# Where the last head keeps the previous head's gated output

## The chip, the cores and the metric

The kernel runs on one core of a Trainium2 chip. Its time is the device time of one launch in microseconds (us). The kernel before took 1392.94 us, the median of three runs (1392.48 to 1395.17).

## The reference

One step of a two-layer decoder on 512 prompt tokens and 32 sample tokens (8 sequences of 4), 544 columns in all, with 1024 features. Layer 0 mixes with a short gated convolution, layer 1 with a retention of four heads; each layer ends with a gated feed-forward network (FFN) of 2816 hidden features. What matters here is the retention of layer 1 and the start of its FFN:

```python
x = x + m                                   # m: the mixer's output
x = x + swiglu(rmsnorm(x, norm_ffn[i]), ffn_w_gate[i], ffn_w_up[i], ffn_w_down[i])
# retention mixer, per head h (dk = 256, dv = 512):
q, k, v, g = jnp.split(x @ w_in, ...)       # q and k then turned by rotary
o, S = retention_chunkwise(q, k, v, s0)     # scores, inner and cross products, new state
of = (o - mean(o)) * rsqrt(var(o) + eps)
out = (silu(g) * of * gn_g) @ w_out         # summed over the heads into x
```

## The kernel before

**Number format.** Every product is made of three matmuls: an operand `a` is split into a high part `ah` (float32r, made by ScalarE, ACT) and a low part `al = a - ah` (made by VectorE, DVE), and `a*b` is `ah*bh + ah*bl + al*bh` on TensorE (PE). The helper `split` (L206 ACT, L207 DVE) does one such split. So each step on PE waits for an ACT instruction and a DVE instruction that follows it.

**Layout.** `x` is kept transposed as 8 tiles of 128 features by 544 columns. Its parts for the products of the retention are `xh[0..7]` and `xl[0..7]`, all in one resident tile `parts`. A projection by an output matrix (`project`, L190) walks over 4 feature tiles ("k tiles") of its input with 6 matmuls each, 24 in all.

**A head.** The loop over `h` in 0..3 starts with `value` (V = x @ w_v from `xh`, `xl`, weights in four pieces c = 0..3, each piece over two of the eight feature tiles: c = 0 reads tiles 0 and 1, c = 1 tiles 2 and 3, and so on). Behind c = 0 PE transposes the last parts of the previous head's normalized output, and DVE multiplies them into that head's gate tile (L1612, L1616): it then holds the gated output of the previous head, `older`. Behind c = 1, `qk_split` splits the keys and queries, `keys` transposes the keys, and `held_parts` splits the gated output of the previous head. Then follow `state`, `scores`, `inner`, the sample updates (L1669, L1687, L1693) and the store of the states. Between these, `fill` puts projections of the previous head's gated output through its output matrix, `held_project(h, n)` for n = 0..7, to give PE work while the other engines prepare. In heads 1 and 2 all eight are done inside the head. In head 3, n = 2, 3, 4, 5 are done inside it, n = 0 and 1 at its end, and n = 6 and 7 inside `last_project`, which projects head 3's own output: in the order 0, 1, 4, 5, 2, 3, 6, 7, with `held_project` ahead of n = 6 and of n = 7. Each n ends with `residual(n)`, the DVE addition into `x[n]` (L318).

**What follows.** `ffn(1)` prepares from each `x[kt]` the seven operand blocks of a Strassen-like product: `operand(kt)` scales `x[kt]` into a tile `f` (L884, ACT), subtracts blocks of `f` (L325 to L333, DVE), and splits the blocks into `oh` and `ol` (L206, L207). It runs over kt in the order 0, 1, 4, 5, 2, 3, 6, 7 after the program's order of the residuals; a pair kt, kt + 4 shares one `f`, and there are two `f` buffers. The first job's products then read `oh[0..3]` and `ol[0..3]` (L426, PE): block 0 and block 1 of all four pairs (24 matmuls), then three products over the first three pairs (27 matmuls), then what needs the fourth pair's rest.

**Memory.** Pools are stacks of tiles; a pool opened after others are closed takes the same addresses, and each of its tiles waits for the tiles that it covers (`reuse_waits="tile"`). Behind the same resident pools lie, in the retention, with bytes per partition from the common base: `vp` (`vyh` and `vyl`, 2 x 8704), `qp` (`qkhl1` 8704, `qkhl0` 8192, `vs` 2048), `kp` (`rot1` 36352 to 40704, `rt0` to 42880, `gt` 42880 to 47232), `tp`, which has its `gate` at 72448 to 81152, and three state tiles `S`; in the FFN: `gu` (4 x 4352), the weight tiles `w2`, `w4`, `h2`, `l2`, `h4`, `l4` (18432 together), the two `f` (35840 to 41280 and 41280 to 46720), then `oh`/`ol` of the pairs, 7616 each, from 46720.

**Where the previous head's split output lies.** `held_parts` writes the high parts to two tiles of `kp`, tags `gt` and `rot1`, and the low parts to `gate` of `tp` (heads 2 and 3). The gated output itself lies in `qkhl1` of `qp` (heads 1 to 3), the same buffer in which `qk_split` puts the split keys; so for heads 2 and 3 (`QAHEAD`) the keys are split after `held_parts` has read the gate tile, while heads 0 and 1 split them first.

**Order.** The program's order is not the order on the engines: a planner places each instruction by the program's order and by when its own cost model finds it ready; each engine then runs its list strictly in that order. `tc.issue_after(ins)` forces an instruction behind another. A `weave` is a generator that `project` advances once after each k tile, so that other work is issued there; `last_product` is the last projection matmul issued so far.

Of the kernel before, what the change touches and what calls it, by code (L numbers as in the profile page):

```python
# [9 lines left out]
F32R = mybir.dt.float32r  # L10
# [3 lines left out]
P = 128  # L14
D = 1024
KT = D // P
SEQ = 512
# [8 lines left out]
NH = 4  # L26
# [18 lines left out]
AHEAD = (1, 2)  # L45

QAHEAD = (2, 3)
# [8 lines left out]
def hybrid_decode_kernel(ctx: ExitStack, tc: tile.TileContext, a: dict, o: dict):  # L56
# [7 lines left out]
    def nm(s):  # L64
        uid[0] += 1
        return f"{s}_{uid[0]}"
# [65 lines left out]
    xh, xl = [[parts[:, i * KT + k, :] for k in range(KT)] for i in range(2)]  # L132
# [72 lines left out]
    def split(dh, dl, src):  # L205
        h = nc.scalar.activation(dh, src, AF.Copy)  # L206
        last_low[0] = nc.vector.tensor_sub(dl, src, dh.bitcast(F32))  # L207
        return h
# [194 lines left out]
    class Job:  # L403
# [10 lines left out]
        weave = iter(())  # L414
# [130 lines left out]
    with ExitStack() as c0:  # L545
# [7 lines left out]
        st = mask_p[:, : KT * NB * 2].rearrange("p (k b s) -> p k b s", k=KT, b=NB)  # L553
# [204 lines left out]
        y = taps(0)  # L758
# [527 lines left out]
    with ExitStack() as c2:  # L1286
# [3 lines left out]
        qp = c2.enter_context(tc.tile_pool(name="rtq", bufs=1, reuse_waits="tile"))  # L1290
# [97 lines left out]

        def qk_split(h, st, which):
            r = st["rot"][which]  # L1390
            both = qp.tile([P, 2, 2, SEQ], F32R, tag=f"qkhl{which}", name=nm("qkhl"), bufs=1)
            th, tl = both[:, 0, :, :], both[:, 1, :, :]
            split(th, tl, r[:, :, :SEQ])
            st["qk"[which]] = (th, tl)

# [7 lines left out]
        def value(h, st):  # L1403

            pv = [bank() for _ in range(4)]
            pvs = psum()
            raw = []
            for c in range(4):
                wh, wl = load_piece(a["rtv"][h, c], 2 * DV, keep=raw)
                for k2 in range(2):  # L1410
                    kt = 2 * c + k2
                    cw = slice(k2 * DV, (k2 + 1) * DV)
                    for tt in range(4):
                        ts_, out = token_tiles(tt), pv[tt]
                        nc.tensor.matmul(out, xh[kt][:, ts_], wh[:, cw], start=(kt == 0), stop=False)  # L1415
                        nc.tensor.matmul(out, xh[kt][:, ts_], wl[:, cw], start=False, stop=False)  # L1416
                        last = nc.tensor.matmul(out, xl[kt][:, ts_], wh[:, cw], start=False, stop=(kt == KT - 1))  # L1417
                if c == 0 and "pair" in st:
                    last_product[0] = last
                    st["pair"]()  # L1420
                if c % 2:

                    with tc.issue_after(last.ins):
                        for g in range(4):
                            kt = 2 * c - 2 + g
                            nc.tensor.matmul(  # L1426
                                pvs[g * NS : (g + 1) * NS, 0, :], xs[:, kt, :],
                                raw[kt // 2][:, kt % 2 * DV : (kt % 2 + 1) * DV],
                                start=(c == 1), stop=(c == 3), skip_group_check=True,
                            )  # L1430
                if c == 1:
                    if h not in QAHEAD:
                        with tc.issue_after(last_normal[0].ins) if h else ExitStack():
                            qk_split(h, st, 1)
                    qk_split(h, st, 0)
                    gs = st["gs"] = one.tile([P, NS], F32, tag="gs", name=nm("gs"), bufs=1)
                    nc.vector.tensor_mul(
                        by_sequence(gs), by_sequence(R[:, 1, HT - NS :]), fq[:, h, :].unsqueeze(1).to_broadcast([P, NB, DS])
                    )
                    sample_scores(h, st, pvs[:, 1, :])  # L1440
                    for dt in range(2):
                        qsrc = st["rot"][0][:, dt, SEQ:].rearrange("p (g r s) -> p g r s", g=4, r=2)
                        for r in range(2):
                            nc.vector.scalar_tensor_tensor(
                                qm[:, dt, :, r, 4 * r : 4 * r + 4], qsrc[:, :, r, :], _gamma(h) ** 4,
                                gs.rearrange("p (g r s) -> p g r s", g=4, r=2)[:, :, r, :], op0=ALU.mult, op1=ALU.mult,
                            )
                    keys(h, st, pvs[:, 1, P:])
                    if h:
                        held_parts(h, older)  # L1450
                    if h in QAHEAD:
                        qk_split(h, st, 1)
            v4 = tp.tile([P, 2, DV], F32R, tag="mid", name=nm("v4"), bufs=1)
            nc.scalar.activation(v4[:, 0, :], pvs[:, 0, :], AF.Copy, scale=fv[:, 4, h : h + 1])
            nc.vector.scalar_tensor_tensor(
                v4[:, 1, :], pvs[:, 0, :], fv[:, 4, h : h + 1], v4[:, 0, :].bitcast(F32), op0=ALU.mult, op1=ALU.subtract
            )

            def placed():
                with tc.issue_after(last_product[0].ins) if h in AHEAD else ExitStack():  # L1460
                    for i in range(2):
                        nc.tensor.matmul(pvs[:, 1, :], put, v4[:, i, :], start=(i == 0), stop=(i == 1))
                vt = kp.tile([P, DV], F32R, tag="rt0", name=nm("vt"), bufs=1)
                vs = st["vs"] = qp.tile([P, DV], F32R, tag="vs", name=nm("vs"), bufs=1)
                v2_split[0] = nc.scalar.activation(vt, pvs[:, 1, :], AF.Copy, scale=sign[:, 0:1])
                nc.vector.scalar_tensor_tensor(
                    vs, pvs[:, 1, :], place[:, 1:2], vt.bitcast(F32), op0=ALU.mult, op1=ALU.add
                )

            st["placed"] = placed  # L1470
            if h not in AHEAD:
                placed()
            vh = vp.tile([P, 4, DV], F32R, tag="vyh", name=nm("vh"), bufs=1)
            vl = swapped(h == 1, [P, 4, DV], F32R, "vl")
            for tt in range(4):
                nc.scalar.activation(vh[:, tt, :], pv[tt], AF.Copy, scale=fv[:, tt, h : h + 1])
                nc.vector.scalar_tensor_tensor(
                    vl[:, tt, :], pv[tt], fv[:, tt, h : h + 1], vh[:, tt, :].bitcast(F32),
                    op0=ALU.mult, op1=ALU.subtract,
                )  # L1480
            st["v"] = (vh, vl)
# [50 lines left out]
        def gate_tile(st, n):  # L1532
            return st["gate"][n // 2][:, n % 2, :] if len(st["gate"]) > 1 else st["gate"][0][:, n, :]
# [176 lines left out]
        held = {}  # L1710

        def held_parts(h, st):

            yh = [kp.tile([P, 2, T], F32R, tag=t, name=nm("oldh"), bufs=1) for t in ("gt", "rot1")]
            yl = swapped(h > 1, [P, 4, T], F32R, "oldl")
            for i, t in enumerate(yh):
                c = slice(2 * i, 2 * i + 2)
                split(t, yl[:, c, :], st["gate"][0][:, c, :])
            held["y"] = [t[:, n, :] for t in yh for n in range(2)], [yl[:, n, :] for n in range(4)]

        def held_project(h, n, add=True, single=False, weave=()):

            if n % 2 == 0:
                held["w"] = load_piece(a["rtout"][h - 1, n // 2], 2 * 4 * P, adding=not add and n > 0)
            pt = [bank(), bank()] if single else psum()
            steps = (step() if step else None for step in weave)
            project(pt, *held["w"], n % 2 * 4 * P, *held["y"], last=add, weave=steps)
            if add:
                residual(n, pt)
            else:  # L1730
                held[n] = pt
# [13 lines left out]
        st = qk_places(0)  # L1745
# [4 lines left out]
        older = None  # L1750
        for h in range(NH):
            more = h + 1 < NH

            def fill(place):

                for n in {1: ((0,), (1,), (2,), (3, 4)), 2: ((0,), (1,), (2,), (3, 4)), 3: ((), (2,), (), (3,))}.get(h, ((),) * 4)[place]:
                    held_project(h, n)
                    if n == 0:
                        st["placed"]()
# [60 lines left out]
            if h == 0:  # L1820
                qk_project(h + 1, nxt, 0, 1, inside)
            elif more:
                nc.sync.dma_start(nxt["rot"][0], q_made[h + 1])
                held_project(h, 6, single=True, weave=(None, inside))
                held_project(h, 7)
            else:
                held_project(h, 5, single=True)
                held_project(h, 0, False, single=True, weave=iter((inside,)))
# [127 lines left out]
```

## Time and profile before

| what | value |
|---|---|
| median of three runs | 1392.94 us |
| profiled execution: time, span | 1393.6 us, 1391.8 us |
| mean granted TensorE clock | 0.995 |
| PE busy | 1376.3 us (99%) |
| DVE busy | 1141.3 us (82%) |
| ACT busy | 832.5 us (60%) |
| POOL busy | 216.0 us (16%) |
| head 3's `value` to the end of `last_project` | about 914 to 1017 us |
| first matmuls of `ffn(1)` | 1017.65 us |

The profile page gives busy times, the span in 40 slices of 34.8 us, and the chain of work that ended last. Views of the trace give instructions in order of time (start, duration, engine, line, operation, output<-inputs, and in brackets the idle time before it and what ended it), groups by line, waits, and windows with busy time, granted clock (1.00 is full speed) and DMA share. In groups and timelines `oldh` and `oldl` are the split output of the previous head, `yh` and `yl` that of head 3 itself. A few per cent of the matmul records are missing.

### The profile page before, as it was taken

How to read it: one execution, taken by the hardware profiler on the slowest of the kernel's cores; microseconds unless marked ns; L12 is line 12 of the kernel's file. 1: busy time of each engine (PE TensorE's matmuls, PEld its weight loads, DVE VectorE, ACT ScalarE, POOL GpSimd, SP SyncE). 2: the span in 40 equal slices, each digit the busy share in tenths (PEclk: the TensorE clock that was granted, in tenths of full speed). 3: DMA queues.
4: the chain of work that ended last, by engine and by line, in shares of the span. 5: the costliest groups of instructions: out<-in, count | busy, mean ns of one | idle time of the engine just before them, and what ended most of it. 6: DMA issues, size and time to landing. Idle time of an engine off the chain costs nothing.

```text
span 1391.8 us, 26526 instructions
## 1 busy us (share of the span) xinstructions
PE 1376.3 (99%) x10396; PEld 1313.6 (94%) x10396; DVE 1141.3 (82%) x1938; ACT 832.5 (60%) x1304; POOL 216.0 (16%) x255
## 2 busy tenths in 40 slices
PE   9999999999999999999999999999979999999998
PEld 9999999999999999999977787877979999999998
DVE  6998889888989878789877666676779898988875
ACT  7666567776677557676642413222567767667654
POOL 0111012121222104111110000000111222221212
PEclk9999999999999999999999999999989999999999
DMA  6566347777776745678666655556736767777752
GB/s 223 122 163 160 110 120 176 155 173 182 153 191 151 173 98 163 182 201 204 185 243 218 207 205 192 205 205 231 194 73 164 171 166 175 153 180 172 160 115 87
DMA packets 100733, 236.69 MB, mean 170 GB/s; under 512 B 9952, under 2 KB 34032, under 8 KB 100096
## 3 DMA queue, kind: packets, MB, share of 16 engines
q1 hardware_dynamic: 68608, 168.37, 37.9%
q0 software_dynamic: 29264, 57.40, 24.1%
q10 hardware_dynamic: 2736, 9.23, 1.7%
q8 instruction: 81, 1.33, 0.4%
q14 instruction: 44, 0.36, 0.1%
HBM read 193.74 MB, written 29.53 MB: 160 GB/s over the span
## 4 chain that ended last, share of the span: by engine, by line
PE 96%; DVE 2%; DMA 1%; ACT 1%; issue 0%; SPq 0%; DVEq 0%; ACTq 0%
PE sm L426 45%; PE mm L426 17%; PE mm L190 14%; PE sm L190 5%; PE sm L1416 2%; PE sm L1417 2%; PE sm L1415 2%; PE sm L178 2%; PE sm L179 1%; PE sm L180 1%; PE sm L1669 1%; DMA x<-in_xT_dram 1%; PE mm L1426 1%; PE mm L1597 1%; PE mm L1687 0%; DVE ol L207 0%
## 5 line engine op out<-in xcount | busy, mean ns | idle before, releaser
L426 PE MATMUL sm<-oh,wh 128*128 128x272 f32 x872 | 252.5, 290 | 6.5 <-ACT oh L206 6.5
L426 PE MATMUL sm<-ol,wh 128*128 128x272 f32 x872 | 252.1, 289 | 1.0 <-DVE ol L207 0.9
L426 PE MATMUL sm<-oh,wl 128*128 128x272 f32 x872 | 251.3, 288 | 0.0
L206 ACT ACTIVATE h<-w 128x512 fp32r<-128x512 f32 (+3 forms) x175 | 141.1, 806 | 92.7 <-PE mm L426 85.8
L207 DVE TENSOR_TENSOR l<-w,h 128x512 fp32r<-128x512 f32 (+3 forms) x175 | 158.4, 906 | 23.7 <-ACT h L206 21.8
L339 ACT ACTIVATE wh<-w 128x1024 fp32r<-128x1024 f32 (+1 forms) x138 | 138.2, 1001 | 62.4 <-PE sm L426 45.4
L426 PEld LDWEIGHTS sm<-oh,wh 128*128 128x128 f32 x872 | 165.1, 189 | 7.4 <-ACT oh L206 7.2
L426 PEld LDWEIGHTS sm<-ol,wh 128*128 128x128 f32 x872 | 164.6, 189 | 1.9 <-DVE ol L207 1.8
L426 PEld LDWEIGHTS sm<-oh,wl 128*128 128x128 f32 x872 | 164.9, 189 | 0.0
L426 PE MATMUL sm<-parts,wh 128*128 128x272 f32 x768 | 148.3, 288 | 0.0
L206 ACT ACTIVATE wh<-w 128x1024 fp32r<-128x1024 f32 (+3 forms) x74 | 63.2, 860 | 126.8 <-PE mm L190 86.7
L342 POOL DMA_DIRECT2D wl<-in_ffgu_dram x87 | 81.3, 935 | 340.6 <-ACT wl L341 161.1
L426 PEld LDWEIGHTS sm<-parts,wh 128*128 128x128 f32 x768 | 120.3, 188 | 0.0
L426 PE MATMUL mm<-oh,h 128*128 128x272 f32 x404 | 116.2, 288 | 0.0
L426 PE MATMUL mm<-oh,l 128*128 128x272 f32 x404 | 115.7, 286 | 0.0
L426 PE MATMUL mm<-ol,h 128*128 128x272 f32 x404 | 115.4, 286 | 0.0
L426 PE MATMUL sm<-parts,wl 128*128 128x272 f32 x384 | 110.4, 288 | 0.0
L341 ACT ACTIVATE wl<-wh 128x512 fp32r<-128x512 f32 (+1 forms) x178 | 106.2, 596 | 2.3
L340 DVE TENSOR_TENSOR wl<-w,wh 128x512 fp32r<-128x512 f32 (+1 forms) x138 | 89.8, 651 | 16.7 <-ACT wh L339 16.5
L426 PE MATMUL sm<-oh,h 128*128 128x272 f32 x292 | 85.7, 294 | 0.0
L426 PE MATMUL sm<-ol,h 128*128 128x272 f32 x292 | 84.9, 291 | 0.0
L426 PE MATMUL sm<-oh,l 128*128 128x272 f32 x292 | 84.6, 290 | 0.0
(395 smaller groups left out, 3795.4 us busy)
## 6 DMA issues: line engine op xcount, KB each, us to landing
w<-in_ffgu_dram SPq DMA_DIRECT2D x66, 512.0 KB
wl<-in_ffgu_dram POOLq DMA_DIRECT2D x87, 256.0 KB, 5.3
S<-in_rets_dram SPq DMA_DIRECT2D x16, 1024.0 KB
out_rets_dram<-S SPq DMA_DIRECT2D x16, 1024.0 KB
w<-in_ffdn_dram SPq DMA_DIRECT2D x36, 384.0 KB
cb<-in_ffgu_dram SPq DMA_DIRECT2D x22, 512.0 KB
w<-in_cvin_dram SPq DMA_DIRECT2D x21, 512.0 KB
wl<-in_ffdn_dram POOLq DMA_DIRECT2D x48, 192.0 KB, 4.7
```

Of the source, the lines that this page charges most:

```text
L178: nc.tensor.matmul(out, lh, rh, start=start, stop=False, skip_group_check=True)
L190: last_product[0] = nc.tensor.matmul(half(pt, hf)[:, :HT], w[:, c], act[k][:, hf * HT : (hf + 1) * HT], start=(first and k == ks[0] and i ...
L206: h = nc.scalar.activation(dh, src, AF.Copy)
L207: last_low[0] = nc.vector.tensor_sub(dl, src, dh.bitcast(F32))
L339: nc.scalar.activation(wh, w, AF.Copy)
L340: last_mixed[0] = nc.vector.tensor_sub(wl[:, :n], w[:, :n], wh[:, :n].bitcast(F32))
L341: minus = nc.scalar.activation(wl[:, n:], wh[:, n:].bitcast(F32), AF.Copy, scale=-1.0)
L342: nc.gpsimd.dma_start(wl[:, n:], src[:, 1, :] if len(src.shape) == 3 else src[:, n:], accum_op=ALU.add)
L426: last = nc.tensor.matmul(out, w[:, c], b, start=(first and j == 0 and i == 0), stop=(j == len(self.ks) - 1 and i == 2), skip_group_check= ...
L1415: nc.tensor.matmul(out, xh[kt][:, ts_], wh[:, cw], start=(kt == 0), stop=False)
L1416: nc.tensor.matmul(out, xh[kt][:, ts_], wl[:, cw], start=False, stop=False)
L1417: last = nc.tensor.matmul(out, xl[kt][:, ts_], wh[:, cw], start=False, stop=(kt == KT - 1))
```

## The change

Three edits in head code.

1. For the last head the keys are split ahead of the queries, as in heads 0 and 1, and not into `qkhl1` but into two tiles of `kp` with the tags `gt` and `rot1`, which in heads 1 and 2 hold the high parts of the previous head's output. The condition `h not in QAHEAD` becomes `h != 2`.
2. For the last head `held_parts` is no longer called behind c = 1 of `value`. It is called in `fill`, ahead of the head's first `held_project` (n = 2, between the two calls of `state`), and it writes in four splits of 544 columns into `xh[0..3]` and `xl[0..3]`, which no later step of the layer reads as x's parts. No tile of `kp` or `tp` holds them then.
3. In heads 1 and 2 the generator given to `held_project(h, 6)` has one more empty step, so that `inside` (the transposes of the third token tile's normalized output, and the last state update) is issued after the third k tile and not after the second.

```diff
         def qk_split(h, st, which):
             r = st["rot"][which]
-            both = qp.tile([P, 2, 2, SEQ], F32R, tag=f"qkhl{which}", name=nm("qkhl"), bufs=1)
-            th, tl = both[:, 0, :, :], both[:, 1, :, :]
+            if which and h == NH - 1:
+                th, tl = [kp.tile([P, 2, SEQ], F32R, tag=t, name=nm("khl"), bufs=1) for t in ("gt", "rot1")]
+            else:
+                both = qp.tile([P, 2, 2, SEQ], F32R, tag=f"qkhl{which}", name=nm("qkhl"), bufs=1)
+                th, tl = both[:, 0, :, :], both[:, 1, :, :]
             split(th, tl, r[:, :, :SEQ])
...
                 if c == 1:
-                    if h not in QAHEAD:
+                    if h != 2:
                         with tc.issue_after(last_normal[0].ins) if h else ExitStack():
                             qk_split(h, st, 1)
                     qk_split(h, st, 0)
...
-                    if h:
+                    if h in AHEAD:
                         held_parts(h, older)
-                    if h in QAHEAD:
+                    if h == 2:
                         qk_split(h, st, 1)
...
         def held_parts(h, st):
 
+            if h == NH - 1:
+                for n in range(4):
+                    split(xh[n], xl[n], gate_tile(st, n))
+                held["y"] = xh[:4], xl[:4]
+                return
...
                 for n in {1: ((0,), (1,), (2,), (3, 4)), 2: ((0,), (1,), (2,), (3, 4)), 3: ((), (2,), (), (3,))}.get(h, ((),) * 4)[place]:
+                    if h == NH - 1 and n == 2:
+                        held_parts(h, older)
                     held_project(h, n)
...
-                held_project(h, 6, single=True, weave=(None, inside))
+                held_project(h, 6, single=True, weave=(None, None, inside))
                 held_project(h, 7)
```

## The prediction

> **What bounds the kernel now.** I read the page first (its slices), then the waits of PE, then PE in order of time around its longest wait, then the granted clock by windows.
>
> ```profile
> PE   9999999999999999999999999999979999999998
> PE sm L426 <- ACT oh L206: 6.5, 3, 5.5
> PE sm L426 <- DVE ol L207: 0.9, 2, 0.7
> PE sm L1597 <- DVE yn L1574: 0.4, 2, 0.2
> ```
>
> PE is the bound nearly everywhere; only slice 30 (1009 to 1044 us) has a hole. 7.4 us of PE's waits are for `oh` and `ol`, the operands of `ffn(1)`, and 0.4 us for the third token tile's normalized output in heads 1 and 2. Inside head 3 PE waits for nothing that this view lists. So a change to heads can pay or cost in three places: at the two waits of 0.2 us, in new waits, or at the hand-over from `last_project` to `ffn(1)`. That place in order of time, then by windows:
>
> ```profile
> 1017.00 0.41 PE L190 MATMUL mm<-yh,wl 128*128 128x272 f32 x2
> 1017.65 0.40 PE L426 MATMUL sm<-oh,wh 128*128 128x272 f32 x1 [0.24 <-ACT oh L206]
> ...
> 1020.09 0.29 PE L426 MATMUL sm<-oh,l 128*128 128x272 f32 x1
> 1025.92 0.59 PE L426 MATMUL sm<-oh,wh 128*128 128x272 f32 x1 [5.54 <-ACT oh L206]
> ...
> 1026.00:1035.70 9.70, 8.69 (x32) 7.41 (x33) 8.91 (x17) 6.67 (x11) 0.00 (x0) 0.50 0.06 11
> 1035.70:1046.00 10.30, 10.30 (x86) 10.30 (x85) 7.66 (x14) 5.12 (x8) 2.09 (x2) 1.00 0.50 130
> ...
> 1021.00:1022.00 1.00, 0.00 (x0) 0.00 (x0) 1.00 (x3) 1.00 (x3) 0.00 (x0) 1.00 0.02 2
> 1022.00:1023.00 1.00, 0.00 (x0) 0.00 (x0) 1.00 (x2) 1.00 (x2) 0.00 (x0) 0.52 0.00 0
> ```
>
> A window row gives PE, weight loads, DVE, ACT, POOL (busy us), then clock, DMA share, GB/s. The longest wait costs more than its 5.54 us: the clock falls about 1.6 us after the last matmul ends (1020.38 to 1022.0) and stays at 0.50 until 1035.7. PE's 8.69 busy us there would be 4.35 at full clock. The hand-over therefore loses 7.4 + 4.35 = **11.75 us**.
>
> Why are the operands late? Views by tile of `oldh` and of x, the timeline of ACT, and the chain of waits:
>
> ```profile
> L190 PE MATMUL mm<-oldh,wl x48: 285/288/291, 947.4 to 1014.1; 128*128 128x272 f32 x48
> 990.35 0.79 DVE L318 TENSOR_TENSOR x<-x,sm 128x272 f32<-128x272 f32 x2 [1.10 <-PE sm L190]
> L318 DVE TENSOR_TENSOR x<-x,mm x7: 714/721/722, 993.4 to 1017.4; 128x544 f32<-128x544 f32 x7
> 1014.19 1.06 ACT L339 ACTIVATE wh<-w 128x1024 fp32r<-128x1024 f32 x1 [4.91 <-PE mm L190]
> 1015.15 0.73 ACT L884 ACTIVATE f<-x,vec 128x544 f32<-128x544 f32 x1
> 1029.12 0.64 DVE ol L207
> 1029.81 1.27 PE sm L426 x4
> ```
>
> `x[0]` is final at 991.14, yet its first scaling into `f` starts at 1015.15, 24 us later and right behind the last matmuls on `oldh` (1014.1). The buffers explain it: `f` lies at 35840 to 41280 and 41280 to 46720, over `rot1` and `gt` of `kp`, which hold `oldh`; `ol` of the second pair and `oh` of the third lie over `gate` of `tp`, which holds `oldl`. All are read by `held_project(3, 7)`. From there the chain runs through ACT and DVE until PE resumes.
>
> **The change, part by part.**
>
> *Buffers (edits 1 and 2).* In head 3 `gt` and `rot1` then hold split keys, last read by the scores, and `gate` of `tp` is last read in head 2. The moved work is the groups of 1014.5 to 1036 us; the room is the window ahead:
>
> ```profile
> L207 DVE TENSOR_TENSOR ol<-f,oh 128x544 fp32r<-128x544 f32 (+1 forms) x12 | 9.2, 814 | 0.7 <-ACT oh L206 0.7
> L325 DVE TENSOR_TENSOR f<-f 128x272 f32<-128x272 f32 x4 | 1.8, 438 | 0.7 <-ACT f L884 0.7
> L206 ACT ACTIVATE oh<-f 128x544 fp32r<-128x544 f32 (+1 forms) x12 | 8.2, 722 | 0.9 <-DVE f L333 0.7 <-DVE f L325 0.2
> L884 ACT ACTIVATE f<-x,vec 128x544 f32<-128x544 f32 x8 | 5.6, 736 | 0.3 <-DVE ol L207 0.3
> 991.00:1017.00 26.00, 26.00 (x210) 26.00 (x208) 13.65 (x21) 14.00 (x19) 3.32 (x5) 1.00 0.66 151
> L206 ACT ACTIVATE oh<-f x12: 639/658/884, 1017.0 to 1032.2; 128x544 fp32r<-128x544 f32 x8, 128x816 fp32r<-128x816 f32 x4
> L207 DVE TENSOR_TENSOR ol<-f,oh x12: 717/720/1008, 1018.1 to 1032.9; 128x544 fp32r<-128x544 f32 x8, 128x816 fp32r<-128x816 f32 x4
> 1045.87 10.23 PE sm L426 x82
> ```
>
> DVE's operand work is 9.2 us of low parts and four groups of four subtractions like L325's, 16 x 0.438 = 7.0: 16.2 in all. ACT's is 8.2 + 5.6 = 13.8. Only `x[7]`'s must follow the last residual: on DVE 1.0 + 0.72 + 3 x 0.43 = 3.0, on ACT 0.73 + 0.88 + 0.66 = 2.3. So 13.2 us of DVE and 11.5 of ACT can move ahead, into 26 us in which DVE is busy 13.65 and ACT 14.0. That makes 26.9 and 25.5: just full. A backlog of 0 to 2 us at the end of the projections (1017.4) is likely.
>
> What then stands behind the end? `x[7]`'s residual ends 0.8 us after it (1017.4 + 0.72 = 1018.1). Then in sequence scaling 0.73, two subtractions 0.7, high parts 0.88 and 0.66, the second low part 0.72: 4.5 us after the end, 5.6 if the split of the next weights (1.06 as at 1014.19) goes first on ACT. PE has 24 + 27 = 51 matmuls that do not need it, at 10.23 / 82 = 0.125 us: 6.4 us of cover. With a backlog of 0 to 2, PE waits 0 to 1.2 there. The first matmuls need the third and fourth pair's first blocks, where the same backlog comes a second time: 0 to 2. I take **1.5 us left**; without any cover at all the chain costs 5.6 plus a clock fall of 4.35.
>
> *Crowding of the projections.* ACT's splits of weights now share the queue with operands. The tightest is the piece for `held_project(3, 6)`, whose low part is finished by a transfer:
>
> ```profile
> 996.01 0.86 POOL L215 DMA_DIRECT2D wl<-in_rtout_dram  x1 [4.58 <-ACT wl L214]
> wl<-in_rtout_dram POOLq DMA_DIRECT2D x3, 512.0 KB, 7.8
> 1005.18 0.41 PE L190 MATMUL mm<-oldh,wh 128*128 128x272 f32 x2
> ```
>
> 996.0 + 7.8 = 1003.8 against 1005.2: 1.4 us of slack, against one operand instruction ahead of it (0.73). Cost 0 to 1; I take **0.3**.
>
> *Head 3's splits (edit 2).* The eight instructions have the shape of `yh`'s, and the best gap lies behind c = 3's weights:
>
> ```profile
> 985.93 2.30 ACT L206 ACTIVATE yh<-gate 128x544 fp32r<-128x544 f32 x4 [5.11 <-DVE gate L1612]
> 986.62 2.63 DVE L207 TENSOR_TENSOR yl<-gate,yh 128x544 fp32r<-128x544 f32 x4 [0.72 <-ACT yh L206]
> 940.64 0.69 ACT L1476 ACTIVATE vh<-sm,fv 128x512 fp32r<-128x512 f32 x1 [4.62 <-PE sm L1417]
> 941.36 0.75 DVE L1477 SCALAR_TENSOR_TENSOR vl<-sm,fv,vh 128x512 fp32r<-128x512 f32 x1 [4.08 <-ACT vh L1476]
> 946.93 0.41 PE L190 MATMUL mm<-oldh,wh 128*128 128x272 f32 x2
> 948.07 0.68 DVE L207 TENSOR_TENSOR mid<-sm,mid 128x512 fp32r<-128x512 f32 x1
> 924.30 2.12 ACT L206 ACTIVATE oldh<-gate 128x1088 fp32r<-128x1088 f32 x2 [4.66 <-DMA S<-in_rets_dram]
> ```
>
> `xh[0..3]` are last read at c = 1, so the splits are ready before the idle 936.0 to 940.6 on ACT and to 941.4 on DVE: 2.30 and 2.63 us fit into 4.6 and 4.1. That cover hides them. Placed behind the state's splits instead (as the program has them), the first part would be ready at 948.75 + 0.66 = 949.4 and PE, due at 946.9, would wait 2.5 us unless the next state matmuls go first. 0 to 2.5; I take **0**, since the planner fills gaps with what is ready. The keys' split moves into ACT's 4.66 us ahead of 924.30: cost 0. It waits for `held_project(2, 7)`, and behind it on ACT stands only `value`'s work of c = 1. Head 3's own gate load takes `qkhl1` when the older gate is split and not when the scores are done: earlier, cost 0.
>
> *Edit 3.* One k tile is 6 x 0.125 = 0.75 us:
>
> ```profile
> 908.48 0.52 PE L190 MATMUL sm<-oldh,wh 128*128 128x272 f32 x2
> ...
> 910.84 0.29 PE L190 MATMUL sm<-oldh,wh 128*128 128x272 f32 x1
> 911.34 0.63 PE L1597 MATMUL sm<-cb,yn 128*128 128x128 f32 x4 [0.22 <-DVE yn L1574]
> ```
>
> Up to 910.84 (the rows left out hold two each, 0.25 us apart) there are already 19 matmuls ahead of the transposes, one more than three k tiles. So the planner had them there, and the edit binds little. It gains 0 to 0.4 (two waits of 0.22); if the last update came later by a tile it would cost up to 0.75 each. I take -0.2.
>
> **Sum.** -11.75 + 1.5 + 0.3 + 0 - 0.2 = -10.15. The profiled execution took 1393.6 (span 1391.8 and 1.8 around it), 0.66 above the median; it would be 1383.45. Against the median: 1392.94 - 10.15 = **1382.8 us**. About 0.2% (2.8 us) is what can be told from no change.
>
> **Rivals.**
>
> *B, the clock still falls.* If the order on ACT and DVE leaves one wait of about 3 us at the hand-over, over the 1.6 us after which the row at 1022 shows 0.52, the half-clock stretch is paid again: 7.4 - 3 = 4.4 gained, **1388.5**. For it: both engines are just full. Against it: 6.4 us of cover. The Trainium skill ("TensorE: Matmul & The Clock Gate", Part 1) lets the clock fall after an idle window of about 3.4 us and return after 3.4 us of sustained work. By that rule the half-clock stretch would cost only 3.4 / 2 = 1.7 us and B would end at 1385.9 (an estimate from that page); the trace disagrees, with 9.7 us at 0.50, though that stretch has waits in it.
>
> *C, no gain: the queue's head.* Before the first `f`, ACT waits 4.91 us with the weights' split at 1014.19, whose own buffer is freed by the same late projection. If that instruction stays ahead of `f` in ACT's list, nothing starts earlier: **1392.9**. For it: the present order. Against it: the planner put `f` there because its buffer was not free, and it makes the list anew. The Trainium skill ("TensorE: Matmul & The Clock Gate", Architectural detail, on engine queue depths) calls ACT's and DVE's queues strictly first in, first out, which speaks for C; the trace agrees, with 4.91 us in which ACT does nothing while x is ready.
>
> *D, slower: DVE becomes the bound of the projections.* Two PSUM buffers serve them, each 24 x 0.125 = 3.0 us, and the residual that frees one is a DVE instruction. If operand work stands ahead of residuals and its waits cannot be filled, the 13.2 us do not fit but add to PE's path: 13.2 - 11.75 = 1.5 lost, and one PE wait above 1.6 us adds 4.35. Midway: **1396**. It decides from the point at which 90% of the moved work fails to fit. Against it: residuals and weights come first in the program's order.
>
> **How the numbers follow.** The forecast 0.64 (own range 1380 to 1386: leftovers 0 to 4, transposes -0.8 to 0), B 0.18, C 0.09, D 0.09. Range 1379.8 to 1390: the forecast's best end (11.75 + 0.8 = 12.55 gained gives 1380.4, a little less for refills of PE after each wait), and B with a wait of 4.5. Faster by over 0.2%: 0.64 + 0.18 and a little of C, 0.84; within 0.2%: 0.07; slower: 0.09.
>
> **What would show it.** `f<-x` (L884) first at 991 to 1000 us and not at 1015; PE's waits for `oh` and `ol` under 2 us in total; clock 1.00 through the hand-over; DVE and ACT over 23 of the 26 us ahead of it; the 544-column splits of the older gate at 930 to 941 and `held_project(3, 2)` without a wait. Wrong would be: L884 still behind the weights' split (C), a window at 0.50 (B), or the last projections longer than 26 us (D).

## The result and the profile after

The changed kernel takes **1381.18 us** (median of four runs, 1380.74 to 1381.72), beside 1393.91 us for the kernel before on the same chip (1392.48 to 1395.17). The ratio is 0.9909, with a 95% interval of 0.9892 to 0.9926. The forecast was 1382.8 us, with a range of 1379.8 to 1390. The profiled execution took 1381.29 us, with a span of 1379.5. One execution of a kernel below (the transposes behind the fourth k tile, second run) took 1856.8 us at a mean granted clock of 0.67; it was in a slow state and is left out of that kernel's numbers.

First the profile page of the changed kernel (busy time, then the slices of PE and of the granted clock), then its view of the waits of PE (us in total, times, longest):

```profile
PE 1371.1 (99%) x10396; PEld 1309.9 (95%) x10396; DVE 1141.0 (83%) x1940; ACT 831.9 (60%) x1306; POOL 216.0 (16%) x255
PE   9999999999999999999999999999999999999998
PEclk9999999999999999999999999999999999999999
```

```profile
PE sm L577 <- DVE expo L111: 1.1, 1, 1.1
PE sm L1600 <- DVE yn L1577: 0.4, 2, 0.2
PE sm L1419 <- DVE wl L207: 0.4, 1, 0.4
PE mm L190 <- DVE parts L226: 0.3, 1, 0.3
```

The hole in slice 30 is gone, and so are the 7.4 us of waits for `oh` and `ol`. The waits at L1419 and L226 come and go in the kernels of the experiments, with the gain and without it.

The hand-over from `last_project` to `ffn(1)`, in order of time on PE and by windows (PE, weight loads, DVE, ACT, POOL, then clock, DMA share, GB/s):

```profile
1017.24 0.41 PE L190 MATMUL mm<-yh,wl 128*128 128x272 f32 x2
1017.49 0.29 PE L426 MATMUL sm<-oh,wh 128*128 128x272 f32 x1
```

```profile
991.00:1017.40 26.40, 26.40 (x214) 26.40 (x213) 23.31 (x42) 22.99 (x32) 3.89 (x5) 1.00 0.66 152
1017.40:1026.00 8.60, 8.60 (x70) 8.49 (x69) 8.41 (x15) 6.92 (x12) 1.19 (x2) 1.00 0.55 123
1026.00:1035.70 9.70, 9.70 (x82) 9.70 (x81) 8.75 (x15) 6.42 (x12) 2.83 (x3) 1.00 0.52 138
```

The first product of `ffn(1)` follows the last projection without a gap, and the clock stays at 1.00. From the end of the last projection to the end of the span the kernel before needed 1391.8 - 1017.41 = 374.4 us and the changed one 1379.5 - 1017.65 = 361.9 (each end is the start of the last L190 row plus its 0.41): **12.5 us** less. Up to that point the changed kernel is 0.24 us later. So the whole gain lies behind the heads that the diff edits.

ACT and DVE around it, in order of time:

```profile
991.49 0.75 ACT L884 ACTIVATE f<-x,vec 128x544 f32<-128x544 f32 x1 [0.89 <-DVE x L318]
...
1013.14 1.38 ACT L884 ACTIVATE f<-x,vec 128x544 f32<-128x544 f32 x2
1014.44 1.06 ACT L339 ACTIVATE wh<-w 128x1024 fp32r<-128x1024 f32 x1
...
1019.48 0.74 ACT L884 ACTIVATE f<-x,vec 128x544 f32<-128x544 f32 x1
```

```profile
1018.47 0.71 DVE L318 TENSOR_TENSOR x<-x,mm 128x544 f32<-128x544 f32 x1
1021.72 1.64 DVE L207 TENSOR_TENSOR ol<-f,oh 128x816 fp32r<-128x816 f32 x2
```

Seven of the eight scalings into `f` now stand ahead of the weights' split (L339, 1014.44) that headed ACT's queue before, and ACT no longer stands idle ahead of it. Behind the end of the projections (1017.65) are left `x[7]`'s chain, done at 1023.36, and ahead of it the last splits of other operands.

### The profile page after: what moved, and what is told of

It is laid out like the page before. It is cut to its first block, busy times and chain, and to the rows that moved or that the text cites. A ratio compares the mean times of both kernels' runs of the same rounds, so it can differ in the third digit from the quotient of the medians.

```text
span 1379.5 us, 26535 instructions
## 1 busy us (share of the span) xinstructions
PE 1371.1 (99%) x10396; PEld 1309.9 (95%) x10396; DVE 1141.0 (83%) x1940; ACT 831.9 (60%) x1306; POOL 216.0 (16%) x255
## 4 chain that ended last, share of the span: by engine, by line
PE 98%; DMA 1%; DVE 1%; ACT 0%; SPq 0%; issue 0%; DVEq 0%; ACTq 0%
PE sm L426 46%; PE mm L426 17%; PE mm L190 15%; PE sm L190 5%; PE sm L1419 2%; PE sm L1420 2%; PE sm L1418 2%; PE sm L178 2%; PE sm L179 1%; PE sm L180 1%; PE sm L1672 1%; DMA x<-in_xT_dram 1%; PE mm L1429 1%; PE mm L1600 1%; PE mm L1690 1%; DMA w<-in_rtv_dram 0%
## 5 line engine op out<-in xcount | busy, mean ns | idle before, releaser
L339 ACT ACTIVATE wh<-w 128x1024 fp32r<-128x1024 f32 (+1 forms) x138 | 138.1, 1001 | 56.5 <-PE sm L426 45.4
```

What stands on the lines that cost most here:

```text
L339: nc.scalar.activation(wh, w, AF.Copy)
```

## The experiments

**One part alone.** The kernel before, with nothing but the new place of the older gate's parts. The keys stay in their own buffer and are split late, and the transposes stay.

```diff
         def held_parts(h, st):
+            if h == NH - 1:
+                for n in range(4):
+                    split(xh[n], xl[n], gate_tile(st, n))
+                held["y"] = xh[:4], xl[:4]
+                return
```

> The kernel before with one part of the change: in head 3 the older gated output is split over x's parts, at the place where the kernel before splits it (behind chunk c = 1); the keys stay in their own buffer and are split after it as before, and the third tile's transposes stay. Theory M (what counts is that the last projections no longer read the memory that ffn(1)'s operands need): the whole gain, 1381 +- 1 us, first scaling into f at 991 to 992 and no PE wait for oh or ol. Rival K (the earlier, moved split of the keys and the place of the new split give the gain): near before, 1393 +- 1.

Measured: 1381.86 us (1381.62 to 1382.28); ratio to the kernel before 0.9913 (0.9898 to 0.9928). ACT of this kernel in order of time:

```profile
931.54 1.06 ACT L206 ACTIVATE qkhl<-squares 128x1024 fp32r<-128x1024 f32 x1 [0.79 <-DVE parts L207]
...
992.49 0.75 ACT L884 ACTIVATE f<-x,vec 128x544 f32<-128x544 f32 x1 [0.90 <-DVE x L318]
```

The keys are split at 931.5, behind the older gate, and not at 917.7 as in the changed kernel, and the whole gain is there. The place of the keys and of the head's splits is not what pays; that the split output no longer lies under `ffn(1)`'s buffers is.

**Half of the memory, the one and the other way.** In the first kernel the high parts go to `xh` and the low parts stay in the gate buffer of `tp`, which covers `ol` of the second pair and `oh` of the third. In the second the low parts go to `xl` and the high parts stay under `f`.

```diff
+            if h == NH - 1:
+                low = swapped(True, [P, 4, T], F32R, "oldl")
+                for n in range(4):
+                    split(xh[n], low[:, n, :], gate_tile(st, n))
...
+                high = [kp.tile([P, 2, T], F32R, tag=t, name=nm("oldh"), bufs=1) for t in ("gt", "rot1")]
+                high = [t[:, n, :] for t in high for n in range(2)]
+                for n in range(4):
+                    split(high[n], xl[n], gate_tile(st, n))
...
```

> The kernel before with half of the memory freed: the older gate's high parts go over x's parts, its low parts stay in the buffer of the gate that also serves the second pair's low and the third pair's high parts. Theory M with memory as the only gate: the f scalings start at 991, the first pair of operands is ready before the projections end, the rest still waits for the last projection at 1014.1; PE's idle stretch at the hand-over gets shorter by about half, 3 us instead of 5.5, and if the clock still falls some 1.6 us after the last matmul, 1388.5; if it does not fall, 1385. Rival C (order of the queue): the high parts of all pairs stand behind the split of the next weights on ACT and nothing but the scalings moves: 1392 to 1393.5.

> The other half: the older gate's low parts go over x's parts, its high parts stay in the two buffers under f. Theory M with f as the first gate of the chain: nothing starts earlier, 1393 +- 1, with the first scaling at 1015. If the low parts' buffer were the one that counts, 1381 to 1385.

Measured: 1392.26 us for high parts alone (ratio 0.9989, 0.9979 to 0.9998), 1393.68 us for low parts alone (0.9999, 0.9989 to 1.0008). The first kernel's waits of PE and its ACT in order of time:

```profile
PE sm L426 <- ACT oh L206: 5.1, 1, 5.1
```

```profile
992.59 0.75 ACT L884 ACTIVATE f<-x,vec 128x544 f32<-128x544 f32 x1 [0.90 <-DVE x L318]
...
1001.55 0.75 ACT L884 ACTIVATE f<-x,vec 128x544 f32<-128x544 f32 x1
...
1015.58 1.06 ACT L339 ACTIVATE wh<-w 128x1024 fp32r<-128x1024 f32 x1 [4.88 <-PE mm L190]
1016.55 0.64 ACT L206 ACTIVATE oh<-f 128x544 fp32r<-128x544 f32 x1
```

Four scalings do start early, but no `oh` is split before 1016.55, not even the first pair's, whose memory is free (the changed kernel splits it at 992.75). The time is still lost at PE's wait of 5.1 us, so the expected half of the gain did not come. Why the planner put the first pair's `oh` so late, behind the weights' split for which ACT waits 4.88 us, was not tested. In the second kernel the first `f` starts at 1016.18, behind the weights' split, as in the kernel before. Neither half pays with the order that the planner then makes; both together do.

**Free memory, old order.** The changed kernel, with each scaling of `ffn(1)` forced behind the third weights' split of its first job on ACT. `third_split` is that split's last instruction on ACT. Lines of this kernel are shifted by one or two.

```diff
-                nc.scalar.activation(where, halves(x[kt]), AF.Copy, scale=g_ffn(layer, kt))
+                with tc.issue_after(third_split.ins) if layer == 1 else ExitStack():
+                    nc.scalar.activation(where, halves(x[kt]), AF.Copy, scale=g_ffn(layer, kt))
```

> The changed kernel with one order added: each scaling into f of ffn(1) must come behind the third split of the next weights on ACT (the one that waits for the last use of its own buffer, 1014.4), so the memory is free but the queue's order is that of before. Theory Q (memory frees, but the gain comes only because the planner then puts the scalings ahead of that split; the queue's head decides): the whole gain is lost, 1392 to 1394, with the wait for oh of 5 to 6 us and the granted clock at 0.50 behind it. If free memory alone were enough: 1381 to 1383.

Measured: 1393.87 us (ratio 1.0001, 0.9991 to 1.0010). Its waits of PE, then its ACT in order of time:

```profile
PE sm L427 <- ACT oh L207: 6.6, 3, 5.5
```

```profile
1014.91 1.06 ACT L340 ACTIVATE wh<-w 128x1024 fp32r<-128x1024 f32 x1 [4.88 <-PE mm L190]
1016.00 0.63 ACT L342 ACTIVATE wl<-wh 128x512 fp32r<-128x512 f32 x1
1016.54 1.38 ACT L886 ACTIVATE f<-x,vec 128x544 f32<-128x544 f32 x2
```

The 5.5 us wait is back to the tenth. Six x tiles are ready all through ACT's idle 4.88 us, a seventh from 1012.86 on, and the memory that was under the older gate is free; still ACT stands idle ahead of an instruction that waits for something else. So **the queue's order is the last link**: the freed memory pays only because the planner, seeing it free, moves the scalings ahead of that split.

**How much cover is left.** The changed kernel with four, and with nine, multiplications by one on DVE behind the scaling of `x[7]`; the values stay the same.

```diff
+                for _ in range(4 if layer == 1 and kt == KT - 1 else 0):   # 9 in the other kernel
+                    nc.vector.tensor_mul(where, where, ones[:, 0:1].unsqueeze(1).to_broadcast([P, 2, HT]))
```

> The changed kernel with the chain behind the last residual made longer: four exact multiplications by one on DVE (0.64 us each, 2.6 in all) on the scaled x[7] of ffn(1). In the changed kernel the last low part ends 0.66 us before PE needs it, so PE should wait 2.6 - 0.66 = 1.9 us at about 1024. If the clock falls some 1.6 us after the last matmul, as at 1022 in the kernel before, a stretch at 0.50 follows and up to 4.35 us more are lost: 1381.2 + 1.9 = 1383.1 without a fall, up to 1387.5 with it. By the Trainium skill (TensorE: Matmul & The Clock Gate, Part 1: an idle window of about 3.4 us) there is no fall: 1383.1. If the cover of x[7] were larger than the trace says: 1381.2.

> The same with nine multiplications (5.8 us): PE waits about 5.1 us at 1024, near the 5.54 of the kernel before. By the trace of before the clock falls and stays at 0.50 for about 9 us of PE's work: 1381.2 + 5.1 + 4.35 = 1390.7. By the Trainium skill's page on the clock gate (back at full clock after 3.4 us) it would be 1381.2 + 5.1 + 1.7 = 1388.0. Without a fall 1386.3.

Measured: 1385.07 us with four (1383.76 to 1385.70), 1388.18 with nine (1388.06 to 1389.24). The profiled execution with four is the fastest of its runs (span 1382.0, 2.5 us above the changed kernel's). Its waits of PE:

```profile
PE mm L260 <- POOL rN L256: 0.7, 1, 0.7
...
PE sm L426 <- DVE l L207: 0.5, 1, 0.5
...
PE sm L426 <- ACT h L206: 0.2, 1, 0.2
```

None of these is the expected wait. The added 2.99 us (0.75 each, not the 0.64 assumed) are half hidden at `x[7]`'s own operands: between 1024.73 and 1026.41 PE starts six matmuls 0.21 to 0.41 us apart instead of 0.125, a loss of 0.9 us in gaps too short for the view. The rest comes back later as waits for weights and for the next norm, whose DVE work was pushed back by the same amount. The clock stays at 1.00 in this execution. The other three took 0.8 to 1.9 us more; they have no trace, but their mean granted clocks (0.998 to 1.000) are like those of the changed kernel (0.998 to 0.999) and not like those with nine (0.996 to 0.997), so a fall of the clock is an unlikely reason. With nine, PE's longest wait and the windows around it:

```profile
1028.56 1.20 PE L426 MATMUL sm<-oh,h 128*128 128x272 f32 x2 [3.27 <-ACT oh L206]
```

```profile
1024.71:1028.12 3.41, 0.58 (x5) 0.36 (x3) 3.24 (x7) 0.49 (x1) 0.00 (x0) 1.00 0.00 0
1028.12:1031.53 3.41, 2.96 (x9) 2.37 (x10) 3.18 (x5) 1.97 (x5) 0.00 (x0) 0.50 0.02 5
1031.53:1034.94 3.41, 3.41 (x17) 3.41 (x17) 3.16 (x6) 2.36 (x4) 0.00 (x0) 0.50 0.00 0
```

PE waits 3.27 us and not 5.1, since it has other matmuls until 1025.3. That idle stretch brings the clock down, for 6.83 us (1028.12 to 1034.94). The loss of 7.0 us is the 3.27 and half of the 6.4 busy us at 0.50, 3.2; the rest of 0.5 was not taken apart. It comes close to the price of rival B (1388.5, with a wait of about 3 us).

**The late place of the splits.** The changed kernel with the older gate's splits forced behind the state's splits on ACT and on DVE.

```diff
                     if h == NH - 1 and n == 2:
-                        held_parts(h, older)
+                        with tc.issue_after(mid_split[0].ins), tc.issue_after(last_low[0].ins):
+                            held_parts(h, older)
...
```

> The changed kernel with head 3's split of the older gate put behind the state's splits on ACT and DVE, where the program's text has it. The prediction priced this place at 2.5 us of PE wait unless the planner puts other matmuls first. Expected: PE has a wait for parts ahead of held_project(3, 2), 0 to 2.5 us, 1381.2 to 1383.7; if the planner's cover works, 1381.2 +- 0.7.

Measured: 1382.12 us (1380.61 to 1382.99; ratio 0.9912, 0.9897 to 0.9927), no different from the changed kernel. ACT and PE in order of time:

```profile
947.12 2.30 ACT L206 ACTIVATE parts<-gate 128x544 fp32r<-128x544 f32 x4
```

```profile
947.88 0.46 PE L190 MATMUL mm<-parts,wh 128*128 128x272 f32 x2
948.18 0.40 PE L179 MATMUL sm<-vl,knh 128*128 128x512 f32 x1
...
949.12 0.41 PE L190 MATMUL mm<-parts,wh 128*128 128x272 f32 x2
```

The splits run 22 us later and PE does not wait: the planner puts the state's own matmuls between the first ones of `held_project(3, 2)`. The 2.5 us of the prediction's upper bound are not paid in either place.

**The third edit.** One kernel is the changed one without it, the other moves the transposes one k tile further, behind the fourth. The second was run twice.

```diff
-                held_project(h, 6, single=True, weave=(None, None, inside))
+                held_project(h, 6, single=True, weave=(None, inside))                # without
+                held_project(h, 6, single=True, weave=(None, None, None, inside))    # behind the fourth
```

> The changed kernel without its last edit (the third tile's transposes one k tile earlier again, as in the kernel before). Every engine's list of instructions comes out in the same order as that of the changed kernel, so the edit does nothing: 1381.2 +- 0.5, with the two waits of 0.22 us for yn in both. It also stands for the changed kernel in this comparison. The prediction's -0.2 for the edit (0 to -0.8) would put it at 1381.4 to 1382.

> The changed kernel with the third tile's transposes one k tile later still (behind the fourth). If the two waits of 0.22 us for yn are taken away and nothing else is late: 1381.2 - 0.8 to 1381.2 - 0.4 = 1380.4 to 1380.8. If the last update then comes late by a tile (0.75 us in each of two heads): up to 1382.7. If the slack of the update covers it and the waits are hidden anyway: 1381.2 +- 0.4.

> The transposes behind the fourth k tile, beside the kernel that stands for the changed one on the same chip. The trace of the first run shows both waits for yn gone and about 1.1 us less lost by PE in heads 1 and 2, so 1.1 us below that kernel: 1380.1. If the first difference was scatter between executions: equal within 0.4 us.

Measured: without the edit 1381.66 us (1381.19 to 1382.54). Behind the fourth tile 1380.03 us (1379.56 to 1381.41) the first time, and on the chip of the kernel without the edit 1379.47, 1379.88 and 1380.20. PE in order of time without the edit, then behind the fourth tile (first run; both in head 2):

```profile
911.80 0.63 PE L1600 MATMUL sm<-cb,yn 128*128 128x128 f32 x4 [0.23 <-DVE yn L1577]
912.35 0.50 PE L1690 MATMUL mm<-vs,kns 32*128 32x512 f32 x2
```

```profile
910.97 0.60 PE L1600 MATMUL sm<-cb,yn 128*128 128x128 f32 x4
911.50 0.76 PE L1690 MATMUL mm<-vs,kns 32*128 32x512 f32 x4
```

The edit as made changes nothing: the lists of all engines are the same with and without it, and the wait stays. Behind the fourth tile both waits are gone, and the group at L1690 runs in one piece. On one chip each of these three runs is faster than each of the four without it, by 1.8 us between the medians (1381.66 and 1379.88). The intervals of the two ratios to the kernel before (0.9906, 0.9891 to 0.9921; 0.9891, 0.9871 to 0.9911) overlap, so the times place the size of the gain only at some 1 to 2 us. The traces place it better: from the first matmul of `held_project(1, 6)` to the last row of the projections (L190) PE takes 184.22 us in the changed kernel and 184.26 without the edit, but 182.80 and 182.78 behind the fourth tile, 1.4 to 1.5 us less. It is **the fastest version of this study**.

## Why the prediction was right, and where it was off

**The cause** was right, and each link of it was shown: the memory (the one part alone), that neither half of it is enough (the two halves), and the order of ACT's queue (free memory, old order). Open is only why the planner held back the first pair's `oh` when the high parts alone were moved. Rival C was a real mechanism: 1393.87 us where it was priced at 1392.9. It did not come about here because the new list no longer has the split at its head.

**The time** came within 1.6 us of the forecast, in part by chance. The sum gave a gain of 10.15 us, and the medians differ by 12.73; but the sum started from a median of 1392.94, and with one more run that kernel's median is 1393.91. From there the same sum would have been 2.6 us off.

**The gain at the hand-over** was put at 11.75 us and measured 12.5. What was too small is the price of the waits. The view counts a wait from the modelled end of the matmul before, 0.29 us after its start, while at pace PE starts the next one after 0.125; and behind a wait the second matmul follows the first only after 0.23 us at full clock. The kernel before around its second wait, and where its clock is back:

```profile
1018.86 0.40 PE L426 MATMUL sm<-ol,wh 128*128 128x272 f32 x1 [0.69 <-DVE ol L207]
1019.09 0.29 PE L426 MATMUL sm<-oh,wl 128*128 128x272 f32 x1
1019.22 0.29 PE L426 MATMUL sm<-oh,wh 128*128 128x272 f32 x1
...
1035.77 0.29 PE L426 MATMUL sm<-oh,wl 128*128 128x272 f32 x1
```

Counted from start to start, the 13 steps from the last projection's matmul (1017.12) to 1025.92 take 8.80 us where 1.63 would do at pace: 7.2 lost, against the 6.5 that the view lists as waits. The 32 steps from there to 1035.77 take 9.85 where 4.0 would do: 5.85 lost, against 4.35 for the clock and 1.0 for waits. So 13.0 us were lost, not 11.75, and the half-clock term itself was about right. The changed kernel loses some 0.5 us of it again in short gaps up to 1038. The missing part was named at the lower end of the prediction's range ("a little less for refills of PE after each wait") but had no term in the sum.

**What is left at the hand-over** was put at 1.5 us and is about 0.2 (PE starts two matmuls late at 1020.55). The backlog came once and not twice: `x[7]`'s residual starts at 1018.47, 0.8 us after the last projection's end at 1017.65, and the low parts end at 1023.36, 5.7 us after it: the 4.5 of the working, the 0.8, and 0.4 of small gaps. The 51 matmuls that do not need them cover 6.4. DVE and ACT were not "just full": 23.31 and 22.99 of 26.4 us, against 26.9 and 25.5 of 26 in the sum. The working moved every operand instruction except `x[7]`'s ahead of the end, but some of the other pairs' stayed behind it, under cover (the low parts ahead of 1021.72). The cover is soft too: with 2.99 us more on the chain PE lost only 0.9 us there, and the rest fell on later work.

**Crowding** was put at 0.3. The changed kernel's waits list nothing for that piece; the heads end 0.24 us later, which is within what executions differ by.

**Head 3's splits**, cost 0: right, but not at the place named. The prediction saw the gap from 936.0 to 941; the planner put all four splits ahead of it, each as soon as the gate was there and its x tile read for the last time:

```profile
917.66 1.07 ACT L206 ACTIVATE khl<-squares 128x1024 fp32r<-128x1024 f32 x1 [5.27 <-PE mm L190]
...
924.73 1.21 ACT L206 ACTIVATE parts<-gate 128x544 fp32r<-128x544 f32 x2 [4.71 <-DVE gate L1615]
926.29 0.66 ACT L206 ACTIVATE parts<-gate 128x544 fp32r<-128x544 f32 x1 [0.35 <-PE sm L1419]
929.09 0.66 ACT L206 ACTIVATE parts<-gate 128x544 fp32r<-128x544 f32 x1 [2.14 <-PE sm L1419]
```

What was wrong is the place, "930 to 941": the splits were indeed "ready before the idle 936.0", and the planner did not keep them for that gap but put them where they became ready. The keys' split sits where it was expected, in a gap, at no cost.

**The third edit** was put at -0.2 and is 0. The row that says so stood in the prediction: 19 matmuls lay ahead of the transposes already, one more than the edit asks for. The conclusion "binds little" should have been "binds nothing".

**Rival D** (DVE becomes the bound) is out: the last projections take no longer, and DVE has 3.1 us to spare in them. **Rival B** did not happen, since no wait of that length was left.

**The clock** was misread, though it cost the sum nothing. The prediction took from one row that the clock falls about 1.6 us after the last matmul. The kernel before by windows of 3.41 us, set to end where its clock falls (1022.03):

```profile
1018.62:1022.03 3.41, 1.52 (x10) 1.30 (x10) 3.41 (x9) 3.41 (x6) 0.00 (x0) 1.00 0.53 81
1022.03:1025.44 3.41, 0.00 (x0) 0.00 (x0) 3.31 (x7) 3.08 (x6) 0.86 (x1) 0.50 0.14 17
1025.44:1028.86 3.42, 2.14 (x7) 1.51 (x7) 3.42 (x8) 3.20 (x6) 0.00 (x0) 0.50 0.35 62
1028.86:1032.27 3.41, 3.20 (x11) 2.55 (x12) 3.29 (x6) 2.21 (x5) 0.00 (x0) 0.50 0.00 0
1032.27:1035.68 3.41, 3.41 (x17) 3.41 (x17) 2.73 (x5) 1.81 (x3) 0.00 (x0) 0.50 0.00 0
```

The stretch at 0.50 lasts 13.65 us, four windows, and it ends behind the first window in which PE is busy throughout. With nine multiplications it lasts 6.83 us, two windows, by the same reading, and the clock fell 2.8 us after the last matmul's end (1025.3). The stretches at 1.00 behind them are whole multiples of 3.413 us too: 354.99 us (104) in the kernel before and 348.16 (102) with nine. So 1.6 us was only where a window happened to end. The Trainium skill ("TensorE: Matmul & The Clock Gate", Part 1) has such a free-running window of about 3.4 us; the traces agree with that length, and the prediction's "the trace disagrees" was wrong. They do not agree that the window ahead of a fall is idle (last section). The estimate drawn from that page was off as well: it charged one window at half clock, where four were paid: an idle one, two with waits in them and the full one that ends the stretch.

## What to carry to other kernels

When a phase starts late although its inputs are ready, ask which memory its first outputs lie over and who reads that memory last, and then look at what heads the queue of the engine that would start it: both must be free, and freeing half of the buffers can gain next to nothing. A wait that lets the clock fall is to be priced with its windows, and with further waits while the clock is low, since these keep it low. Count a wait from start to start of the matmuls around it: the idle time that a view lists was 0.3 us short for each wait here. An edit to the program's order is worth nothing where the planner's list already satisfies it; compare the lists before you give it a gain.

## What the runs showed of the hardware that was not expected

A window need not be empty to bring the clock down. In the kernel before PE was busy for 1.52 of 3.41 us in the window ahead of the fall, and with the low parts alone in `xl` for 1.61 (1019.09 to 1022.50). Behind a window with 1.84 busy us near its end (1383.85 to 1387.26) the kernel before kept 1.00. To come back at the hand-over the clock took a full window: those at 0.50 with 2.96 and 3.20 busy us did not bring 1.00 back, and those with 3.41 did. The edges of these windows are inferred from the falls and returns themselves, and the busy times rest on modelled ends of the matmuls.
